# Expert layer on one core: tiles with one half of each factor, and 32 places instead of 64 for the longest list's second block

## The chip, the core and the metric

One core of a Trainium2 chip runs the whole program in one launch. The metric is the device time in microseconds (us), the median of several executions; lower is better. Engines are named as in the profile: PE is TensorE (PEld its loader of stationary operands), DVE VectorE, ACT ScalarE, SP the SyncE queue that issues nearly all transfers.

## The reference

Two layers of a backbone over 256 latent and 256 context tokens of width 1024. Layer 0 ends in a dense feed-forward part, layer 1 in eight experts of which each latent token takes two. The change touches the experts alone:

```python
def moe_swiglu(h, router, w1, w3, w2):
    logits = jnp.einsum('bld,de->ble', h, router).astype(F32)
    top_val, top_idx = lax.top_k(logits, TOP_K)
    top_w = jax.nn.softmax(top_val, axis=-1)
    gate = jnp.sum(jax.nn.one_hot(top_idx, N_EXPERTS, dtype=F32) * top_w[..., None], axis=-2)
    out = jnp.zeros(h.shape, F32)
    for e in range(N_EXPERTS):
        out = out + gate[..., e:e + 1] * swiglu(h, w1[e], w3[e], w2[e])
    return out.astype(h.dtype)
```

`swiglu` is (silu(h w1) * (h w3)) w2 with w1 and w3 of 1024 x 3584 and w2 of 3584 x 1024, all in fp32. The router of the reference, evaluated on its inputs, gives experts 0 to 7 lists of 53, 55, 63, 44, 38, 68, 48 and 143 tokens.

## The kernel before

**Stages.** Layer 0, the mixers of layer 1, then the experts (`experts`, L1302), which run alone at the end. Eight slots each take one expert: slot 0 is expert 0, slots 1 to 7 are the others by falling length of their lists. A slot gathers its tokens into columns (`gather`, L999) and runs seven steps; a step is one chunk of 512 hidden columns.

**Weights.** Every step needs six tiles of 128 x 2048 fp32 (1 MB): two for w1, two for w3 (tile 2 wi + kh holds the half kh of the contraction for factor wi), two for w2 (tile 4 + n holds output half n). They come from memory through a ring of nine buffers in the order of use (`raw`, L142), issued by SP. Nine are fetched before the stage starts (L1321). Every expert's weights are fetched whole: 8 x 7 x 6 = 336 tiles.

**Two ways to multiply.** `CAPS` and `SHORT` (L37, L38) say how many places a slot has, and `ORDER` and `ORDER_SHORT` in which sequence the steps of the slots run. Which of the two is taken is decided on the chip from the lists' lengths (L897 to L901, L1348).

- *Paired* slots (64 places; in `SHORT` slots 0 and 3 to 7) multiply in plain fp32 straight from the fetched tiles: the 64 columns of w1 and of w3 run side by side on two halves of the array (`up_pair`, L1107, matmul at L1113), a transpose and silu follow (`hidden_pair`, L1116), and the two output halves again run side by side (`down_pair`, L1128, L1134). Each fp32 matmul is two instructions in the trace.
- *Split* slots (slot 1 with blocks of 128 and 64 places, slot 2 with 128) multiply in three fp32r products. Each tile is first split into a high and a low part, in two halves of 1024 columns (`split`, L158: ACT at L170 makes the high part, DVE at L171 the low one); buffers for four such halves rotate. `up` (L1137, L1147) runs 12 matmuls per tile for a block of 128 places, and 8 for a block of 64, whose high and low activations lie side by side as one stationary operand of 128 columns. `hidden` (L1150) transposes and splits the result, `down` (L1177, L1184) multiplies by w2.

In the loop of `slots` (L1189) the second product of a step is issued inside the next step: after the first half of that step's first product comes `hidden` of the step before, then `ahead(…, 4, 5)`, which fetches and splits the two w2 tiles (where a split step is followed by a paired one), then the rest. The order on each engine's queue is set when the program is built, partly by a scheduler that moves instructions past each other. Each engine works its queue in order. Slot 1's second product is folded from two halves of rows by a matmul with a 0/1 matrix (`fold`, L1166).

Of the kernel before, what the change touches and what calls it, by code (L numbers as in the profile page):

```python
# [18 lines left out]
P = 128  # L19
# [10 lines left out]
NE = 8  # L30
# [40 lines left out]
NTA = P * len(_TA)  # L71
_TR = {n: i * P for i, n in enumerate(("iota", "iota64", "fold"))}
NTR = P * len(_TR)
# [9 lines left out]
class Net:  # L83
# [57 lines left out]

    def raw(self, src, n=2048):  # L142
# [718 lines left out]
    def route(self, l):  # L861
# [34 lines left out]
        nc.vector.tensor_add(ln, tot[:, 0], tot[:, 1])  # L896
        long = mk("long", [P, NE + 1])  # L897
        nc.vector.scalar_tensor_tensor(long[:, :NE], ln, 64.0, tab[:, P + 24:P + 32], ALU.is_gt, ALU.mult)
        nc.vector.reduce_sum(long[:, NE:], long[:, :NE], AX.X)
        self.long = mk("longi", [P, 1], I32)  # L900
        nc.vector.tensor_copy(self.long, long[:, NE:])  # L901

# [79 lines left out]
    def places(self, s, base, width):  # L982

        nc, mo = self.nc, self.mo
        G = mo.tile([P, 2, P], F32, tag="G", name=self.nm("G"), bufs=2)
        sp = mo.tile([P, 4], F32, tag="spb" if s == 1 else "sp", name=self.nm("spb"),
                     bufs=2 if s == 1 else 3)
        for tt in range(2):
            at = self.spos[tt][s]
            if base:  # L990
                nc.vector.tensor_scalar(sp[:, tt:tt + 1], at, float(-base), None, ALU.add)
                at = sp[:, tt:tt + 1]
            nc.vector.tensor_scalar(G[:, tt], self.t("iota" if width == P else "iota64"), at, None, ALU.is_equal)
        return G, sp

    def gather(self, s, base, width, first=False, whole=False):
# [7 lines left out]
        if whole:  # L1004
            xs = [mo.tile([P, KT, 64], F32, tag="xn", name=self.nm("xn"), bufs=2)]
        else:
            xs = [mo.tile([P, KT, P], F32R, tag=f"x{i}{big}{width if big else ''}", name=self.nm("xg"),
                          bufs=1 if big else 2) for i in range(2 if width == P else 1)]
        nk = 512 // width

        def activations(part):
            pool, tag = (self.hpp, "h") if part and first else (aux, "x")
            px = pool.tile([P, 512], F32, tag=tag, name=self.nm("px"))
            for k in range(nk):
                kk = part * nk + k
                for tt in range(2):
                    nc.tensor.matmul(px[:, k * width:(k + 1) * width], self.X[:, kk, NL + tt * P:NL + (tt + 1) * P],  # L1017
                                     G[:, tt, :width], start=tt == 0, stop=tt == 1)
            v = px.rearrange("p (k c) -> p k c", k=nk)
            sl = slice(part * nk, (part + 1) * nk)  # L1020
            if whole:
# [75 lines left out]
    def part(self, expert, j, i):  # L1097

        if isinstance(expert, int) and (j, i) in self.pre:
            return self.pre.pop((j, i))  # L1100
        return self.raw(self.I["moe"][expert, j, i])

    def parts(self, s, expert, j, i):
# [24 lines left out]
    def down_pair(self, expert, j, h, y):  # L1128

        mm = self.nc.tensor.matmul  # L1130
        ws = [self.part(expert, j, 4 + n) for n in range(2)]
        for f in range(4):
            for n in range(2):
                mm(y[64 * n:64 * n + 64], h[:, f], ws[n][:, f * 512:(f + 1) * 512],  # L1134
                   start=j == 0 and f == 0, stop=j == NCH - 1 and f == 3)
# [14 lines left out]
    def hidden(self, acts):  # L1150
# [24 lines left out]
    def down(self, s, expert, j, n, parts, y, first, last):  # L1175

        mm = self.nc.tensor.matmul  # L1177
        ws = self.parts(s, expert, j, 4 + n)
# [11 lines left out]
    def slots(self, l, steps, order, caps, base=0, first=False):  # L1190
# [60 lines left out]
        for i, (s, j) in enumerate(steps):  # L1251
# [20 lines left out]
            if split:  # L1272
                self.up(s, order[s], j, 0, 1, blocks, pss)
                for ps, b in zip(pss, blocks):
                    a = mo.tile([P, 512], F32, tag="act", name=self.nm("act"), bufs=4)
                    nc.scalar.activation(a, ps, AF.Silu if len(b[0]) > 1 else AF.Copy)
                    acts.append([a])
# [5 lines left out]
                for a, ps, b in zip(acts, pss, blocks):  # L1283
                    if len(b[0]) > 1:
                        nc.vector.tensor_mul(a[0], a[0], ps)
                    else:
                        a.append(mo.tile([P, 512], F32, tag="act", name=self.nm("act"), bufs=4))
                        nc.vector.tensor_copy(a[1], ps)
            else:
                self.up_pair(order[s], j, 1, blocks[0][0][0], pss[0])  # L1290
# [17 lines left out]
    def experts(self, cx, l, ps):  # L1308
# [38 lines left out]

        long = nc.values_load(self.long[0:1, 0:1], min_val=0, max_val=NE + 2)  # L1348
        with tc.If(long < 3, preferred_fallthrough_block=True) as c:
# [71 lines left out]
def _constants():  # L1421
# [10 lines left out]
    for name, d in (("r64", 64), ("r32", 32)):  # L1432
# [6 lines left out]
        tab[:, _TA[name]:][:, :P] = r  # L1439
    tr[:, _TR["iota64"]:][:, :P] = i[None, :] % 64  # L1440
    tr[:, _TR["fold"]:][:, :64] = i[:, None] % 64 == np.arange(64)[None, :]
    ts[:, P:P + 8] = np.arange(8)
    ts[:, P + 8:P + 16] = [1e7, 700, 600, 500, 400, 300, 200, 100]
# [114 lines left out]
```

## Time and profile before

| | |
|---|---|
| median of 3 runs | 1982.26 us (1972.82 to 1993.71) |
| the profiled execution, its own time | 1975.04 us |
| its span, first to last instruction | 1973.2 us |
| mean granted clock of TensorE | 0.982 |
| expert stage in the span, first gather to the last product | 984.5 to 1950 us |
| transfers in the program | 478.45 MB, 242 GB/s over the span |

The span is what the rows below divide; 1.84 us of the execution lie around it. Times in a row of the timeline are from the span's start. A row of the timeline gives start, length, engine, line, operation, tiles and the number of instructions merged; the length runs to the end of the last one, so the step from one row's start to the next row's is what the work occupies on PE.

### The profile page before, as it was taken

The numbers are of one execution on the slowest core, as the hardware profiler recorded it, in microseconds if no ns is written. First come the engines' busy times: TensorE is split into PE (matmuls) and PEld (weight loads), VectorE is DVE, ScalarE is ACT, GpSimd is POOL, SyncE is SP. The second block draws the span as 40 slices with busy tenths as digits, with TensorE's granted clock in tenths as the row PEclk, the third lists the DMA queues.
The fourth block names the chain that finished last, engine by engine and source line by source line (L and its number), as shares of the span: only waits on it lengthen the run. The fifth ranks groups of instructions, "written<-read, shape, count | busy, mean of one in ns | idle before, by whom it ended". The sixth has DMA issues, their size and how long they took to land.

```text
span 1973.2 us, 22813 instructions
## 1 busy us (share of the span) xinstructions
PE 1883.8 (95%) x8918; PEld 1177.6 (60%) x8918; DVE 835.8 (42%) x1633; ACT 665.4 (34%) x1059; POOL 0.2 (0%) x4
## 2 busy tenths in 40 slices
PE   6999999999999999999699999999999999998995
PEld 4866546778888878665656545454455455444552
DVE  6586455533333347865423323322342223223262
ACT  4475234422222225854322312221332223212231
POOL 0000000000000000000000000000000000000000
PEclk9999999999999999999899999999999999999998
DMA  7320345442332224225578987998998998998972
GB/s 301 137 76 22 118 186 217 159 150 74 122 108 79 72 91 171 98 108 202 217 286 336 364 347 296 420 418 331 421 404 345 420 375 318 409 368 328 418 306 81
DMA packets 68811, 478.45 MB, mean 242 GB/s; under 512 B 7760, under 2 KB 8912, under 8 KB 13392
## 3 DMA queue, kind: packets, MB, share of 16 engines
q1 hardware_dynamic: 68112, 473.04, 61.0%
q10 hardware_dynamic: 576, 3.80, 0.5%
q8 instruction: 74, 1.21, 0.2%
q14 instruction: 49, 0.40, 0.1%
HBM read 475.76 MB, written 1.05 MB: 242 GB/s over the span
## 4 chain that ended last, share of the span: by engine, by line
PE 93%; DMA 3%; DVE 2%; ACT 1%; issue 0%; SPq 0%; ACTq 0%; DVEq 0%
PE ph L1113 17%; PE ph L1147 11%; PE y L1134 8%; PE pf L184 6%; PE pf L186 6%; PE pf L185 6%; PE y L1184 6%; PE pp L186 3%; PE pp L185 3%; PE pp L184 3%; PE ada L211 2%; PE px L1017 2%; PE ds L664 2%; PE po L184 1%; DMA raw<-in_ada 1%; PE po L185 1%
## 5 line engine op out<-in xcount | busy, mean ns | idle before, releaser
L171 DVE TENSOR_TENSOR w<-raw,w 128x1024 fp32r<-128x1024 f32 (+2 forms) x310 | 353.4, 1166 | 295.5 <-ACT w L170 295.1
L170 ACT ACTIVATE w<-raw 128x1024 fp32r<-128x1024 f32 (+2 forms) x310 | 302.5, 1009 | 287.3 <-PE pf L186 152.6
L1113 PE MATMUL ph<-raw,xn 128*64 128x512 f32 x1344 | 354.4, 608 | 0.0
L1147 PE MATMUL ph<-w,xg 128*128 128x512 f32 x896 | 224.8, 403 | 4.1 <-DVE w L171 4.1
L1113 PEld LDWEIGHTS ph<-raw,xn 128*64 128x64 f32 x1344 | 99.5, 138 | 182.5 <-issue 179.8
L1147 PEld LDWEIGHTS ph<-w,xg 128*128 128x128 f32 x896 | 165.6, 190 | 63.2 <-issue 15.3
L1134 PE MATMUL y<-raw,hn 128*64 128x512 f32 x672 | 173.8, 601 | 0.0
L184 PE MATMUL pf<-fhhi,w 128*128 128x512 f32 x352 | 137.2, 391 | 1.5 <-ACT fhhi L315 1.5
L185 PE MATMUL pf<-fhlo,w 128*128 128x512 f32 x352 | 137.1, 389 | 0.0
L186 PE MATMUL pf<-fhhi,w 128*128 128x512 f32 x352 | 137.0, 389 | 0.0
L112 ACT ACTIVATE act<-ph 128x512 f32<-128x512 f32 x42 | 25.1, 597 | 279.7 <-PE ph L1113 279.7
L1184 PE MATMUL y<-w,hh 128*128 128x512 f32 x336 | 105.5, 411 | 7.4 <-DVE yacc L1242 3.8
L1134 PEld LDWEIGHTS y<-raw,hn 128*64 128x64 f32 x672 | 52.2, 138 | 93.9 <-issue 92.8
L184 PE MATMUL pp<-hhi,w 128*128 128x512 f32 (+1 forms) x272 | 104.0, 382 | 0.0
L186 PE MATMUL pp<-hhi,w 128*128 128x512 f32 (+1 forms) x272 | 102.8, 378 | 0.0
L185 PE MATMUL pp<-hlo,w 128*128 128x512 f32 (+1 forms) x272 | 101.7, 374 | 0.0
L1125 DVE TENSOR_TENSOR hn<-hn,ht 128x256 f32<-128x256 f32 x42 | 17.6, 418 | 190.6 <-ACT hn L1124 190.6
L1184 PEld LDWEIGHTS y<-w,hh 128*128 128x128 f32 x336 | 61.4, 190 | 43.6 <-issue 16.0
L184 PEld LDWEIGHTS pf<-fhhi,w 128*128 128x128 f32 x352 | 66.0, 188 | 18.4 <-issue 2.5
L185 PEld LDWEIGHTS pf<-fhlo,w 128*128 128x128 f32 x352 | 66.1, 188 | 13.8 <-DVE fhlo L316 0.3
L186 PEld LDWEIGHTS pf<-fhhi,w 128*128 128x128 f32 x352 | 66.1, 188 | 13.8
L185 PE MATMUL pf<-ulo,w 128*128 128x512 f32 x176 | 68.5, 389 | 0.0
(326 smaller groups left out, 2440.9 us busy)
## 6 DMA issues: line engine op xcount, KB each, us to landing
raw<-in_moe SPq DMA_DIRECT2D x336, 1024.0 KB, 8.9
raw<-in_ada SPq DMA_DIRECT2D x45, 1024.0 KB, 4.9
raw<-in_ffn SPq DMA_DIRECT2D x22, 1024.0 KB, 4.8
raw<-in_win SPq DMA_DIRECT2D x16, 1024.0 KB, 4.8
raw<-in_ffn SPq DMA_DIRECT2D x16, 704.0 KB, 4.0
raw<-in_wout SPq DMA_DIRECT2D x8, 1024.0 KB, 4.9
raw<-in_winv SPq DMA_DIRECT2D x7, 640.0 KB, 4.8
raw<-in_ada ACTq DMA_DIRECT2D x3, 1024.0 KB, 7.7
```

The costliest lines, as they stand in the source:

```text
L170: self.nc.scalar.activation(hi[:, :m], t[:, c:c + m], AF.Copy)
L171: self.nc.vector.tensor_sub(lo[:, :m], t[:, c:c + m], hi[:, :m].bitcast(F32))
L184: mm(out, llo, rhi, start=first, stop=False)
L185: mm(out, lhi, rlo, start=False, stop=False)
L186: mm(out, lhi, rhi, start=False, stop=last)
L211: nc.tensor.matmul(st["ps"][32 * j:32 * j + 32, :], self.sc[:, k, :], w[:, j * 512:(j + 1) * 512], start=k == 0, stop=k == KT - 1)
L664: nc.tensor.matmul(ps[:, :w], q[j][r:r + 32, q0:q0 + P], k[j][r:r + 32, k0:k0 + w], start=True, stop=True, tile_position=(r, 0))
L1017: nc.tensor.matmul(px[:, k * width:(k + 1) * width], self.X[:, kk, NL + tt * P:NL + (tt + 1) * P], G[:, tt, :width], start=tt == 0, stop=t ...
L1113: mm(ps[64 * wi:64 * wi + 64], x[:, 4 * kh + kk], ws[wi][:, kk * 512:(kk + 1) * 512], start=kh + kk == 0, stop=kh == 1 and kk == 3)
L1134: mm(y[64 * n:64 * n + 64], h[:, f], ws[n][:, f * 512:(f + 1) * 512], start=j == 0 and f == 0, stop=j == NCH - 1 and f == 3)
L1147: mm(ps, xs[x][:, 4 * kh + kk], ws[kk // 2][i][:, kk % 2 * 512:(kk % 2 + 1) * 512], start=kh == 0 and (x, i, kk) == todo[0], stop=kh == 1 ...
L1184: mm(yn, hs[x][:, f], ws[f // 2][i][:, f % 2 * 512:(f % 2 + 1) * 512], start=first and (x, i, f) == todo[0], stop=last and (x, i, f) == to ...
```

## The change

1. `SHORT` gives the second block of slot 1 32 places instead of 64. That block's products are no longer split: four plain fp32 matmuls of 32 stationary columns run side by side on four strips of the array, one for each of four slices of the contraction, from the fetched tile itself. Their four partial results stand below one another and are summed by the fold (now four strips onto 32 columns). Block one of slot 1 (128 places) still uses the split parts of the same tile, so a tile of slot 1 is now in use until the four plain matmuls have read it.
2. A tile of a paired slot now holds half of the slices of both factors (or of both output halves): two pieces of 128 x 1024 from two tiles of the old layout, 4 KB per partition each. Layout in memory is unchanged; so are the bytes and the count of transfers.
3. The choice of the order also asks whether a list is longer than 160 (then it takes `CAPS`). A table of 128 columns is added.

```diff
-SHORT = ((64,), (128, 64), (128,), (64,), (64,), (64,), (64,), (64,))
+SHORT = ((64,), (128, 32), (128,), (64,), (64,), (64,), (64,), (64,))
...
-        self.dq().dma_start(t[:, :n], src)
+        dst = t[:, :n]
+        if shape:
+            dst = dst.rearrange("p (a c) -> p a c", a=shape[0])
+        self.dq().dma_start(dst, src)
...
+        nc.vector.tensor_scalar(long[:, NE:2 * NE], ln, float(sum(SHORT[1])), 3.0, ALU.is_gt, ALU.mult)
...
+        if width == 32:
+
+            xs = [xs[0][:, :, :32].bitcast(F32), None, None]
+        nk = min(512 // width, KT)
...
     def parts(self, s, expert, j, i):
 
-        return self.ready.pop((s, j, i), None) or self.split(self.part(expert, j, i))
+        if (s, j, i) in self.ready:
+            return self.ready.pop((s, j, i))
+        t = self.part(expert, j, i)
+        return t, self.split(t)
+
+    def both(self, expert, j, i):
+
+
+        if isinstance(expert, int) and (j, i) in self.pre:
+            return self.pre.pop((j, i))
+        w = self.I["moe"][expert, j]
+        h = slice(i % 2 * 1024, (i % 2 + 1) * 1024)
+        src = w[i // 2:i // 2 + 3:2, :, h] if i < 4 else w[4:6, :, h]
+        return self.raw(src.rearrange("w p c -> p w c"), shape=(2, 1024))
 
     def up_pair(self, expert, j, kh, x, ps):
 
         mm = self.nc.tensor.matmul
-        ws = [self.part(expert, j, 2 * wi + kh) for wi in range(2)]
-        for kk in range(4):
-            for wi in range(2):
-                mm(ps[64 * wi:64 * wi + 64], x[:, 4 * kh + kk], ws[wi][:, kk * 512:(kk + 1) * 512],
-                   start=kh + kk == 0, stop=kh == 1 and kk == 3)
+        for t in range(2):
+            w = self.both(expert, j, 2 * kh + t)
+            for kk in range(2):
+                for wi in range(2):
+                    c = wi * 1024 + kk * 512
+                    mm(ps[64 * wi:64 * wi + 64], x[:, 4 * kh + 2 * t + kk], w[:, c:c + 512],
+                       start=kh + t + kk == 0, stop=kh + t + kk == 3)
...
-        ws = self.parts(s, expert, j, 2 * wi + kh)
+        t, ws = self.parts(s, expert, j, 2 * wi + kh)
         for ps, (xs, *_) in zip(pss, blocks):
+            if len(xs) == 3:
+                for kk in range(4):
+                    mm(ps[32 * kk:32 * kk + 32], xs[0][:, 4 * kh + kk], t[:, kk * 512:(kk + 1) * 512],
+                       start=kh == 0, stop=kh == 1)
+                continue
...
+                if len(a) == 3:
+                    for q in range(2):
+                        for i in range(4):
+                            nc.tensor.matmul(pt[:, q * P + i * 32:q * P + (i + 1) * 32], a[q][:, i * P:(i + 1) * P],
+                                             self.t("fold")[:, 64:96], start=True, stop=True)
+                    h = hh[:, :, :32].bitcast(F32)
+                    v = pt[:, :256].rearrange("p (q f c) -> p q f c", q=2, f=4)
+                    nc.scalar.activation(h, v[:, 0], AF.Silu)
+                    nc.vector.tensor_mul(h, h, v[:, 1])
+                    parts.append((h, None, None))
+                    continue
...
+            if len(hs) == 3:
+                for f in range(4):
+                    mm(yn[32 * f:32 * f + 32], hs[0][:, f], t[:, f * 512:(f + 1) * 512], start=first, stop=last)
+                continue
...
-        pre = {(i // 6, j): self.raw(self.I["moe"][0, i // 6, j]) for i, j in enumerate((0, 2, 1, 3, 4, 5, 0, 2, 1))}
+        pre = {(i // 6, i % 6): self.both(0, i // 6, i % 6) for i in range(9)}
```

`down_pair` is changed as `up_pair` is. Lines of the changed kernel lie some 3 to 43 lines further down: L1113 becomes L1133, L1134 L1156, L1147 L1175, L1159 L1187, L1184 L1227; the plain matmuls of 32 columns are L1169 and L1222.

**Order on PE, first place.** One tile of slot 1 (w3, first half), before: `xg_7397` and `xg_7398` are the high and low activations of the block of 128, `xg_7406` those of the second block, `w_...` a split half of the tile.

```order
L1147 MATMUL ph_8956<-w_8959,xg_7397 128x512 x2
L1147 MATMUL ph_8956<-w_8959,xg_7398 128x512
...
L1147 MATMUL ph_8956<-w_8962,xg_7397 128x512 x2
L1147 MATMUL ph_8956<-w_8962,xg_7398 128x512
...
L1147 MATMUL ph_8957<-w_8959,xg_7406 128x512 x4
L1147 MATMUL ph_8957<-w_8962,xg_7406 128x512 x4
```

The same tile now; `raw_7240` is the fetched tile itself.

```order
L1175 MATMUL ph_8894<-w_8897,xg_7398 128x512 x2
L1175 MATMUL ph_8894<-w_8897,xg_7399 128x512
...
L1175 MATMUL ph_8894<-w_8900,xg_7398 128x512 x2
L1175 MATMUL ph_8894<-w_8900,xg_7399 128x512
...
L1169 MATMUL ph_8895<-raw_7240,xg_7407 32x512 x4
```

Eight matmuls of 128 columns from split parts became four of 32 columns from the raw tile.

**Order on PE, second place.** The end of a step of slot 2 inside the paired step that follows, before: `ht_8697` is the transposed hidden block of slot 2, `hh_8698` its high part made by ACT from it, `w_8707` the first split half of the w2 tile, and `ph_8686` the first product of the paired step.

```order
L1147 MATMUL ph_8620<-w_8654,xg_7804 128x512
L1113 MATMUL ph_8686<-raw_7237,xn_7945 64x512
L1159 MATMUL ht_8697<-tab,act_8618 128x128 x4
L1113 MATMUL ph_8686<-raw_7238,xn_7945 64x512
...
L1184 MATMUL y_8102<-w_8707,hh_8698 128x512 x2
L1184 MATMUL y_8102<-w_8707,hl_8703 128x512
```

The same place now:

```order
L1175 MATMUL ph_8566<-w_8600,xg_7777 128x512
L1133 MATMUL ph_8632<-raw_7238,xn_7918 64x512 x4
L1133 MATMUL ph_8632<-raw_7239,xn_7918 64x512 x4
L1187 MATMUL ht_8643<-tab,act_8564 128x128 x4
L1227 MATMUL y_8075<-w_8653,hh_8644 128x512 x2
L1227 MATMUL y_8075<-w_8653,hl_8649 128x512
```

Before, one of the eight plain matmuls of the paired step stands alone ahead of the transposes, and seven between them and the second product; now all eight stand ahead of the transposes. The program's paired matmuls (1008 in the stage) stand in runs between other work; 86 runs held one without its partner of the other half of the array before, 20 do now. Of the seven steps of slot 2, six had the seven matmuls in between before and the last had none; now none of the seven has any. On ACT the queue is the same in both kernels at this place:

```order
L1319 ACTIVATE act_8564<-ph_8531 128x512
L173 ACTIVATE w_8597<-raw_7237 128x1024
L173 ACTIVATE w_8600<-raw_7237 128x1024
L182 ACTIVATE hh_8644<-ht_8643 128x512
L173 ACTIVATE w_8653<-raw_7240 128x1024
L173 ACTIVATE w_8656<-raw_7240 128x1024
```

These rows are of the changed kernel: the high part of the hidden block is made first, the halves of the w2 tile behind it.

## Rows read from the trace of the kernel before

**Rows 1.** The page, part 1: busy time, share of the span, instructions.

```profile
PE 1883.8 (95%) x8918; PEld 1177.6 (60%) x8918; DVE 835.8 (42%) x1633; ACT 665.4 (34%) x1059; POOL 0.2 (0%) x4
```

**Rows 2.** The page, part 4: the chain that ended last, shares by engine.

```profile
PE 93%; DMA 3%; DVE 2%; ACT 1%; issue 0%; SPq 0%; ACTq 0%; DVEq 0%
```

**Rows 3.** Windows, expert stage: length, busy per engine, clock, DMA share, GB/s.

```profile
984.50:1950.00 965.50, 938.43 (x4178) 492.41 (x4178) 309.31 (x431) 249.55 (x337) 0.00 (x0) 0.98 0.88 356
```

**Rows 4.** Waits of the SP queue: total us, times, longest.

```profile
SPq L149 <- DVE w L171: 669.3, 97, 39.1
SPq L149 <- PE ph L1113: 422.7, 141, 10.5
```

**Rows 5.** Lines by form: busy us, mean ns of one, idle before them.

```profile
L1113 PE MATMUL ph<-raw,xn 128*64 128x512 f32 x1344 | 354.4, 608 | 0.0
L1147 PE MATMUL ph<-w,xg 128*128 128x512 f32 x896 | 224.8, 403 | 4.1 <-DVE w L171 4.1
```

**Rows 6.** Timeline of PE in a step of slot 1: start, us, what.

```profile
1186.76 9.56 PE L1147 MATMUL ph<-w,xg 128*128 128x512 f32 x40
1196.25 3.65 PE L1134 MATMUL y<-raw,hn 128*64 128x512 f32 x16
1199.84 0.50 PE L1147 MATMUL ph<-w,xg 128*128 128x512 f32 x1
```

**Rows 7.** Timeline of PE: four fp32 products of 32 columns side by side, elsewhere.

```profile
919.51 1.06 PE L211 MATMUL ada<-raw,sc 128*32 128x512 f32 x8
920.51 0.66 PE L632 MATMUL ptp<-tab,ap 128*128 128x128 f32 x4
...
926.86 1.92 PE L211 MATMUL ada<-raw,sc 128*32 128x512 f32 x16
```

**Rows 8.** Timeline, second product of slot 2 with plain matmuls ahead of it.

```profile
1266.50 1.07 PE L1113 MATMUL ph<-raw,xn 128*64 128x512 f32 x2
1267.51 0.66 PE L1159 MATMUL ht<-tab,act 128*128 128x128 f32 x4
1268.09 3.65 PE L1113 MATMUL ph<-raw,xn 128*64 128x512 f32 x14
1271.67 0.73 PE L1184 MATMUL y<-w,hh 128*128 128x512 f32 x2
...
1268.69 3.89 ACT L170 ACTIVATE w<-raw 128x1024 fp32r<-128x1024 f32 x4
...
1269.78 4.63 DVE L171 TENSOR_TENSOR w<-raw,w 128x1024 fp32r<-128x1024 f32 x4 [0.26 <-ACT w L170]
```

**Rows 9.** Timeline, the same place in the last step of slot 2.

```profile
1808.09 0.33 PE L1159 MATMUL ht<-tab,act 128*128 128x128 f32 x1
1811.31 0.72 PE L1184 MATMUL y<-w,hh 128*128 128x512 f32 x2 [2.89 <-DVE w L171]
...
1808.95 3.88 ACT L170 ACTIVATE w<-raw 128x1024 fp32r<-128x1024 f32 x4
...
1810.03 4.63 DVE L171 TENSOR_TENSOR w<-raw,w 128x1024 fp32r<-128x1024 f32 x4 [0.25 <-ACT w L170]
```

**Rows 10.** Windows behind that wait, PE alone: length, busy, clock, DMA share, GB/s.

```profile
1812.20:1815.60 3.40, 3.40 (x10) 0.50 1.01 410
```

**Rows 11.** DMA, 1400 to 1450 us: the queue's packets, MB, share of 16 engines.

```profile
q1 hardware_dynamic: 2881, 20.98, 101.1%
```

**Rows 12.** DMA, 867.5 to 868.5 us: a tile with 4 KB per partition.

```profile
DMA packets 104, 0.41 MB, mean 414 GB/s; under 512 B 3, under 2 KB 3, under 8 KB 104
...
q1 hardware_dynamic: 104, 0.41, 101.9%
```

**Rows 13.** The page, part 6: issues, KB each, median us to landing.

```profile
raw<-in_moe SPq DMA_DIRECT2D x336, 1024.0 KB, 8.9
...
raw<-in_win SPq DMA_DIRECT2D x16, 1024.0 KB, 4.8
...
bd<-in_lrubd SPq DMA_DIRECT2D x2, 512.0 KB, 3.7
```

More of the change, by code (lines that the diff above doesn't have):

```diff
@@ L71 @@
 NTA = P * len(_TA)
-_TR = {n: i * P for i, n in enumerate(("iota", "iota64", "fold"))}
+_TR = {n: i * P for i, n in enumerate(("iota", "iota64", "iota32", "fold"))}
 NTR = P * len(_TR)
@@ L140, in dq, with raw @@
         return self.nc.scalar if self.ndq <= 8 and self.ndq % 2 else self.nc.sync
-    def raw(self, src, n=2048):
+    def raw(self, src, n=2048, shape=None):
         if self.ring:
@@ L896, in route @@
         nc.vector.tensor_add(ln, tot[:, 0], tot[:, 1])
-        long = mk("long", [P, NE + 1])
+        long = mk("long", [P, 2 * NE + 1])
         nc.vector.scalar_tensor_tensor(long[:, :NE], ln, 64.0, tab[:, P + 24:P + 32], ALU.is_gt, ALU.mult)
-        nc.vector.reduce_sum(long[:, NE:], long[:, :NE], AX.X)
+        nc.vector.tensor_scalar(long[:, NE:2 * NE], ln, float(sum(SHORT[1])), 3.0, ALU.is_gt, ALU.mult)
+        nc.vector.reduce_sum(long[:, 2 * NE:], long[:, :2 * NE], AX.X)
         self.long = mk("longi", [P, 1], I32)
-        nc.vector.tensor_copy(self.long, long[:, NE:])
+        nc.vector.tensor_copy(self.long, long[:, 2 * NE:])
         pm = mk("pm", [P, 2, NE])
@@ L992, in places @@
                 at = sp[:, tt:tt + 1]
-            nc.vector.tensor_scalar(G[:, tt], self.t("iota" if width == P else "iota64"), at, None, ALU.is_equal)
+            nc.vector.tensor_scalar(G[:, tt], self.t({P: "iota", 64: "iota64", 32: "iota32"}[width]), at, None, ALU.is_equal)
         return G, sp
@@ L1006, in gather @@
         else:
-            xs = [mo.tile([P, KT, P], F32R, tag=f"x{i}{big}{width if big else ''}", name=self.nm("xg"),
+            xs = [mo.tile([P, KT, P], F32R, tag=f"x{i}{big}{max(width, 64) if big else ''}", name=self.nm("xg"),
                           bufs=1 if big else 2) for i in range(2 if width == P else 1)]
-        nk = 512 // width
+        if width == 32:
+            xs = [xs[0][:, :, :32].bitcast(F32), None, None]
+        nk = min(512 // width, KT)
         def activations(part):
@@ L1018, in activations @@
                                      G[:, tt, :width], start=tt == 0, stop=tt == 1)
-            v = px.rearrange("p (k c) -> p k c", k=nk)
+            v = px[:, :nk * width].rearrange("p (k c) -> p k c", k=nk)
             sl = slice(part * nk, (part + 1) * nk)
-            if whole:
+            if whole or width == 32:
                 self.acopy(xs[0][:, sl], v)
@@ L1097, in part, with parts @@
     def part(self, expert, j, i):
+        return self.raw(self.I["moe"][expert, j, i])
+    def parts(self, s, expert, j, i):
+        if (s, j, i) in self.ready:
[3 more added lines that the diff above has]
+    def both(self, expert, j, i):
         if isinstance(expert, int) and (j, i) in self.pre:
             return self.pre.pop((j, i))
-        return self.raw(self.I["moe"][expert, j, i])
-    def parts(self, s, expert, j, i):
-        return self.ready.pop((s, j, i), None) or self.split(self.part(expert, j, i))
+        w = self.I["moe"][expert, j]
+        h = slice(i % 2 * 1024, (i % 2 + 1) * 1024)
+        src = w[i // 2:i // 2 + 3:2, :, h] if i < 4 else w[4:6, :, h]
+        return self.raw(src.rearrange("w p c -> p w c"), shape=(2, 1024))
     def up_pair(self, expert, j, kh, x, ps):
         mm = self.nc.tensor.matmul
-        ws = [self.part(expert, j, 2 * wi + kh) for wi in range(2)]
-        for kk in range(4):
-            for wi in range(2):
-                mm(ps[64 * wi:64 * wi + 64], x[:, 4 * kh + kk], ws[wi][:, kk * 512:(kk + 1) * 512],
-                   start=kh + kk == 0, stop=kh == 1 and kk == 3)
+        for t in range(2):
[5 more added lines that the diff above has]
+                       start=kh + t + kk == 0, stop=kh + t + kk == 3)
     def hidden_pair(self, a):
@@ L1130, in down_pair @@
         mm = self.nc.tensor.matmul
[L1131 to L1135, printed above, removed]
+        for t in range(2):
+            w = self.both(expert, j, 4 + t)
+            for f in range(2):
+                for n in range(2):
+                    c = n * 1024 + f * 512
+                    mm(y[64 * n:64 * n + 64], h[:, 2 * t + f], w[:, c:c + 512],
+                       start=j == 0 and t + f == 0, stop=j == NCH - 1 and t + f == 2)
     def up(self, s, expert, j, wi, kh, blocks, pss):
@@ L1177, in down @@
         mm = self.nc.tensor.matmul
-        ws = self.parts(s, expert, j, 4 + n)
+        t, ws = self.parts(s, expert, j, 4 + n)
         for b, hs in enumerate(parts):
             yn = y(b)
+            if len(hs) == 3:
+                for f in range(4):
+                    mm(yn[32 * f:32 * f + 32], hs[0][:, f], t[:, f * 512:(f + 1) * 512], start=first, stop=last)
+                continue
             todo = [(x, i, f) for x in range(len(hs)) for i in range(2) for f in range(4) if x + i < 2]
@@ L1275, in slots @@
                     a = mo.tile([P, 512], F32, tag="act", name=self.nm("act"), bufs=4)
-                    nc.scalar.activation(a, ps, AF.Silu if len(b[0]) > 1 else AF.Copy)
+                    nc.scalar.activation(a, ps, AF.Silu if len(b[0]) == 2 else AF.Copy)
                     acts.append([a])
@@ L1283, in slots @@
                 for a, ps, b in zip(acts, pss, blocks):
-                    if len(b[0]) > 1:
+                    if len(b[0]) == 2:
                         nc.vector.tensor_mul(a[0], a[0], ps)
@@ L1288, in slots @@
                         nc.vector.tensor_copy(a[1], ps)
+                        if len(b[0]) == 3:
+                            a.append(None)
             else:
@@ L1346, in all_slots @@
             self.finish()
-        long = nc.values_load(self.long[0:1, 0:1], min_val=0, max_val=NE + 2)
+        long = nc.values_load(self.long[0:1, 0:1], min_val=0, max_val=NE + 2 + 9)
         with tc.If(long < 3, preferred_fallthrough_block=True) as c:
@@ L1440, in _constants @@
     tr[:, _TR["iota64"]:][:, :P] = i[None, :] % 64
+    tr[:, _TR["iota32"]:][:, :P] = i[None, :] % 32
     tr[:, _TR["fold"]:][:, :64] = i[:, None] % 64 == np.arange(64)[None, :]
+    tr[:, _TR["fold"] + 64:][:, :32] = i[:, None] % 32 == np.arange(32)[None, :]
     ts[:, P:P + 8] = np.arange(8)
```

## The prediction

> **What bounds the kernel now.** I read the page's engine table first, then the chain, then the expert stage by windows, then the waits of the transfer queue. PE is busy for 95% of the span [rows 1], and the chain of work that ended last is 93% PE and 3% transfers [rows 2]: PE sets the end. The change touches the expert stage alone, and there in 965.5 us PE is busy for 938.4, while the transfers fill 0.88 of the 16 DMA engines' time [rows 3]. So PE bounds the stage, with the transfers close behind. In a full stretch the queue moves 20.98 MB in 50 us, 420 GB/s, at 101.1% of the engines [rows 11]: 2.50 us for a tile of 1.0486 MB, 840 us for 336 tiles. SP mostly waits for a buffer to come free, 669 us in all behind a split on DVE and 423 us behind paired products [rows 4]; a fetched tile is there in time, and the two big groups of PE show idle of 0.0 and 4.1 us [rows 5]. Work taken from PE here can shorten the stage, as long as no new wait appears on PE and the tiles still come.
>
> **The 32 places.** In slot 1 each of 42 tiles (7 steps of 6) had 8 matmuls of 128 columns for the second block. In such a step 40 of them occupy PE from 1186.76 to 1196.25 us [rows 6], 9.49 / 40 = 0.237 us each, 1.90 us per tile. In their place comes a group of four plain fp32 matmuls of 32 columns side by side. The program has that form in another part: a lone group (eight instructions, as an fp32 matmul is two) starts at 919.51 and the next work at 920.51, 1.00 us; two groups in a row take 1.92 us against 1.06 for one, so the second adds 0.86 [rows 7]. In the new order each group stands alone between matmuls of other widths, so I take 1.00. The gain is 0.90 us per tile, 37.7 us for 42 (43.6 with 0.86). The fold keeps its 8 matmuls per step; ACT and DVE lose a few short operations, beside PE's work and worth nothing. The splits stay, as the block of 128 needs them.
>
> The Trainium skill's page "TensorE: Matmul & The Clock Gate" (Part 3, measured speedup) has three products of 32 columns side by side at 2.38 times the speed of one after the other. Four at the same share, 0.79, would by an estimate from that page take 1.08 us where the ideal is 0.86, and the gain would be 34.4 us instead of 37.7. The rows with four side by side decide here.
>
> **Whole pairs.** Paired matmuls share the array: eight of them (16 instructions) run from 1196.25 to 1199.84, 3.59 us or 0.90 per pair [rows 6]. One without its partner takes as long as a pair: the lone one from 1266.50 to 1267.51 took 1.01, and the seven that follow 3.58, from 1268.09 to 1271.67, as much as eight [rows 8]. Where the order tears a pair apart, half a pair's time, 0.45, is lost at each of the two runs. A tile with both factors is enough for whole pairs, so the order has no reason to start one half early: by the count of runs 86 held an odd matmul and 20 do now. 66 x 0.45 = 29.5 us. The bounds are nothing, if the halves that are torn apart fill gaps that PE would have had anyway, and 66 x 0.55 = 36 with a lone one at 1.01.
>
> **What the new order adds.** The second product of a slot 2 step needs the transposed hidden block, of which ACT makes the high part, and the split halves of the w2 tile, which stand behind that operation on ACT's queue in both kernels. Before, PE has cover: after the transposes at 1267.51 the seven plain matmuls run from 1268.09, meanwhile ACT starts on the halves at 1268.69 and DVE at 1269.78, and the product starts at 1271.67 without a wait [rows 8]. The diff does not say so, but in the new order those matmuls stand ahead of the transposes, in all seven steps of slot 2 (second place of the order). The trace before shows the price already, because its last step of slot 2 had no cover: the last transpose at 1808.09, ACT's halves from 1808.95, DVE's from 1810.03, and PE idle for 2.89 us until 1811.31 [rows 9]. One step of seven paid that, now seven do: 6 x 2.89 = 17.3 us. Queued on PE behind the waiting matmul are the rest of the product and the next paired products; ACT waits for those, with nothing else to do.
>
> **The clock.** From 1812.2 to 1815.6 us, behind that wait, the granted clock is 0.50, the lower of its two levels (1.2 of 2.4 GHz), with PE full [rows 10]: 3.4 us for 1.7 us of work. The new waits are alike, so I count 6 x 1.7 = 10.2 us. The bounds are nothing and two such stretches each, 20.4.
>
> **The transfers.** Two things load the queue. First, a tile of slot 1 used to be free once DVE had split it; now four matmuls must have read it too, for a w2 tile those behind the transposes and the fold of the next step. SP issues in order, so all later tiles wait. The trace has no such hold: from below it costs nothing, from above one landing, 8.9 us [rows 13], in each of seven steps, 62 us. Second, 252 tiles come in pieces of 4 KB per partition. A tile of that kind moved 414 GB/s at 101.9% of the engines [rows 12], 2.2% less per busy time than 420 at 101.1%: 2.55 us. From the other side, 512 KB at 4 KB per partition land in 3.7 us and 1024 KB at 8 KB in 4.8 [rows 13]; with 2.50 us of flow in the latter 2.3 are fixed, which leaves 1.4 for half a tile, 2.80 for a whole one. I take 2.55, the direct measure: the queue needs 252 x 2.55 + 84 x 2.50 = 853 us, which the shorter stage of some 935 still covers, with less to spare. Together I take one landing, 9 us, nearer to the lower end, as PE hardly waits for tiles now.
>
> **The sum.** -37.7 - 29.5 + 17.3 + 10.2 + 9 = -30.7 us. Against the profiled execution's own 1975.0 us (its span 1973.2 and 1.8 around) that is 1944. The median of the three runs is 1982.3, 7.2 above that execution, so the predicted median is 1952. A measurement of this kernel tells about 1%, 20 us, from no change: the forecast is outside that, by little.
>
> **Rivals.** *The new waits cost nothing.* While PE stands, the queue fills buffers, and later waits go instead. For it: stretches at the full 420 GB/s [rows 11]. Against it: PE has hardly any such waits now [rows 2], so little can be given back. -37.7 - 29.5 + 9 = -58: 1924. Chance 0.12.
>
> *The torn pairs cost nothing now*, because each odd half fills a gap that stays. For it: the order starts it early only where PE's next work was thought to be waiting. Against it: both parts of the torn pair are followed at once by other work [rows 8]. -30.7 + 29.5 = -1: 1981. Chance 0.14.
>
> *The transfers become the bound.* The two pieces of a tile come from places 1 or 2 MB apart, which no row shows. At 2.80 us a tile the queue is busy for 916 us; with the seven holds of 8.9 us and some 25 us at the stage's ends (nine tiles are there at its start) it needs 1003 us, 38 more than now: 2020. With those stops it is slower than before from (965.5 - 87 - 210) / 252 = 2.65 us a tile on. For it: 0.88 used already. Against it: the 414 GB/s [rows 12]. Chance 0.14. The skill's page "DMA: Bandwidth & Descriptors" (Latency and other measured facts) reports copies whose rows lie 2 MiB apart at 164 GB/s where 214 is full rate; there the distance is between partitions, here between the two pieces of each. By an estimate from that page a tile would take 3.25 us and the kernel some 150 us more; no row here bears it out.
>
> *It does not do what it says.* If the other order ran, slots 0 and 3 would leave the paired way: 72 matmuls of 0.237 against 12 pairs of 0.90, some 6 us in each of 14 steps, 85 us slower. The longest list has 143 tokens, under 160: chance 0.02.
>
> **How the numbers follow.** The forecast, 1952, has 0.58; its own range, with the bounds of the clock, the groups and half of the holds, is 1936 to 1974. The range for 8 in 10 takes in the first two rivals in part: 1922 to 1996; left out are the bound transfers, the other order and the lower half of the first rival. Faster by over 1% (under 1962): the first rival and four fifths of the forecast, 0.60. Slower by over 1% (above 2002): 0.13. Within: 0.27.
>
> **What would show it.** Right: 336 instructions of 32 columns in groups of about 1.00 us; hardly a lone paired matmul left on PE's timeline; seven waits of about 2.9 us before slot 2's second product, ended by the split on DVE, where one was; a lower mean granted clock than 0.982 in the stage; transfers at 0.91 of the engines. Wrong: no such waits, or the clock staying up after them (nearer 1924); PE waiting for paired tiles with the engines full (the pieces cost more); a group above 1.3 us; the same busy time of the paired groups, 354 us in the first product [rows 5], with the pairs whole.

## The result, and the profile after

The changed kernel takes 1944.69 us (median of 4 runs, 1940.58 to 1950.19), the kernel before 1981.51 in the same comparison: ratio 0.9834, 95% interval 0.9802 to 0.9867, by which it is some 33 us faster (the two medians lie 36.8 us apart). The forecast was 1952.

PE's busy time and the chain, from the page of the changed kernel, answer to [rows 1] and [rows 2]:

```profile
PE 1830.0 (94%) x8918; PEld 1122.1 (58%) x8918; DVE 832.3 (43%) x1626; ACT 664.3 (34%) x1052; POOL 0.2 (0%) x4
...
PE 13%; DVE 1%; ACT 0%; issue 0%; DMA 0%; ACTq 0%; DVEq 0%
```

The chain is lost early here (14% of the span in all), so the stage is read by windows instead. The expert stage as [rows 3] has it:

```profile
985.50:1915.10 929.60, 881.31 (x4173) 434.42 (x4175) 305.40 (x423) 248.38 (x330) 0.00 (x0) 0.97 0.93 370
```

It is 35.9 us shorter. PE is busy for 57.1 us less, but idle for 48.3 instead of 27.1, and the transfers fill 0.93 of the engines' time instead of 0.88. Lines by form, PE alone, the first two answer to [rows 5]:

```profile
L1133 PE MATMUL ph<-raw,xn 128*64 128x512 f32 x1344 | 320.5, 601 | 0.0
L1175 PE MATMUL ph<-w,xg 128*128 128x512 f32 x672 | 178.6, 416 | 17.8 <-DVE w L174 17.8
L1227 PE MATMUL y<-w,hh 128*128 128x512 f32 x224 | 81.0, 439 | 18.3 <-DVE w L174 17.6 <-ACT hh L182 0.7
L1169 PE MATMUL ph<-raw,xg 128*32 128x512 f32 x224 | 29.8, 605 | 0.0
```

Paired products cost less; a split matmul costs more (416 ns against 403); idle time stands before the split matmuls of the first product (L1175) and of the second (L1227). A group of four on PE's timeline occupies 0.99 us, 1179.48 to 1180.47:

```profile
1179.48 1.07 PE L1169 MATMUL ph<-raw,xg 128*32 128x512 f32 x8
...
1180.47 0.66 PE L1141 MATMUL ht<-tab,act 128*128 128x128 f32 x4
```

The second product of slot 2, where [rows 8] had cover:

```profile
1124.69 0.66 PE L1187 MATMUL ht<-tab,act 128*128 128x128 f32 x4
...
1125.39 0.60 ACT L182 ACTIVATE hh<-ht 128x512 fp32r<-128x512 f32 x1 [11.05 <-PE ht L1187]
1125.88 3.88 ACT L173 ACTIVATE w<-raw 128x1024 fp32r<-128x1024 f32 x4
...
1128.24 1.22 PE L1227 MATMUL y<-w,hh 128*128 128x512 f32 x2 [2.89 <-DVE w L174]
```

ACT had been waiting for 11 us and makes the halves after the hidden block; PE waits for 2.89 us, as in [rows 9]. Windows of PE behind such a wait, at two of the six places; the granted clock is the third number from the end, half of full speed at the first place and full at the second:

```profile
1263.80:1267.20 3.40, 3.40 (x9) 0.50 1.02 408
1787.20:1790.60 3.40, 3.40 (x15) 1.00 1.02 407
```

What SP waits for, against [rows 4]:

```profile
SPq L152 <- DVE w L174: 646.9, 94, 39.1
SPq L152 <- PE ph L1133: 235.1, 130, 6.1
...
SPq L152 <- PE ph L1169: 88.7, 25, 4.7
SPq L152 <- PE y L1222: 86.8, 12, 11.4
```

The last two are new: 176 us in which the queue stood behind tiles that the plain matmuls of 32 columns still had to read. And a tile is sometimes late:

```profile
1430.38 2.00 ACT L173 ACTIVATE w<-raw 128x1024 fp32r<-128x1024 f32 x2 [3.46 <-DMA raw<-in_moe]
...
1432.84 1.40 PE L1175 MATMUL ph<-w,xg 128*128 128x512 f32 x5 [3.07 <-DVE w L174]
```

### The profile page after: what moved, and what is told of

Its sections match the earlier page's. It is cut to its first block, busy times and chain, and to the rows that moved or that the text cites. A ratio compares the mean times of both kernels' runs of the same rounds, so it can differ in the third digit from the quotient of the medians.

```text
span 1939.3 us, 22842 instructions
## 1 busy us (share of the span) xinstructions
PE 1830.0 (94%) x8918; PEld 1122.1 (58%) x8918; DVE 832.3 (43%) x1626; ACT 664.3 (34%) x1052; POOL 0.2 (0%) x4
## 5 line engine op out<-in xcount | busy, mean ns | idle before, releaser
L1133 PE MATMUL ph<-raw,xn 128*64 128x512 f32 x1344 | 320.5, 601 | 0.0
L1175 PE MATMUL ph<-w,xg 128*128 128x512 f32 x672 | 178.6, 416 | 17.8 <-DVE w L174 17.8
L1133 PEld LDWEIGHTS ph<-raw,xn 128*64 128x64 f32 x1344 | 89.8, 137 | 172.0 <-issue 169.5
L1175 PEld LDWEIGHTS ph<-w,xg 128*128 128x128 f32 x672 | 127.1, 196 | 71.9 <-issue 30.4
L1156 PE MATMUL y<-raw,hn 128*64 128x512 f32 x672 | 155.2, 596 | 0.0
L1145 DVE TENSOR_TENSOR hn<-hn,ht 128x256 f32<-128x256 f32 x42 | 17.6, 418 | 194.2 <-ACT hn L1144 194.2
L1156 PEld LDWEIGHTS y<-raw,hn 128*64 128x64 f32 x672 | 46.4, 137 | 93.0 <-issue 91.1
L1227 PE MATMUL y<-w,hh 128*128 128x512 f32 x224 | 81.0, 439 | 18.3 <-DVE w L174 17.6
L189 PEld LDWEIGHTS pf<-fhhi,w 128*128 128x128 f32 x352 | 66.1, 188 | 13.8
L187 PE MATMUL pf<-uhi,w 128*128 128x512 f32 x176 | 68.5, 389 | 0.0
```

The lines of the kernel that those rows point to most:

```text
L187: mm(out, llo, rhi, start=first, stop=False)
L189: mm(out, lhi, rhi, start=False, stop=last)
L1133: mm(ps[64 * wi:64 * wi + 64], x[:, 4 * kh + 2 * t + kk], w[:, c:c + 512], start=kh + t + kk == 0, stop=kh + t + kk == 3)
L1145: nc.vector.tensor_mul(h, h, v[:, :, 1])
L1156: mm(y[64 * n:64 * n + 64], h[:, 2 * t + f], w[:, c:c + 512], start=j == 0 and t + f == 0, stop=j == NCH - 1 and t + f == 2)
L1175: mm(ps, xs[x][:, 4 * kh + kk], ws[kk // 2][i][:, kk % 2 * 512:(kk % 2 + 1) * 512], start=kh == 0 and (x, i, kk) == todo[0], stop=kh == 1 ...
```

## The experiments

Ratios are to the kernel before, which ran beside each. Runs one to four stood beside one another, so did five to eight and nine to eleven; inside such a group medians are compared, from group to group ratios.

**The changed kernel again.** No edit.

> The changed kernel once more, beside the three that follow, on the same chip. Both theories: 0.983 of the kernel before (0.980 to 0.987), a mean clock near 0.975, six idle times of 2.89 us of PE before the second product of slot 2.

Measured 1947.61 us, before 1974.60: 0.9842 (0.9806 to 0.9878), as expected. The waits before slot 2's second product are the same in its profile, 17.6 us in all.

**Slot 2's high part behind the first w2 tile's split.**

```diff
...
+            if late and len(state[todo[0]]["blocks"]) == 1:
+                n = len(self.acts)
                 ahead(todo[0], todo[1], 4, 5)
+                with self.tc.issue_after(self.acts[n + 1].ins):
+                    todo = hidden(todo)
...
```

`acts` lists the ACT operations of the splits, so that `hidden` comes behind the second half of the first w2 tile; the condition holds for slot 2 alone, which has one block.

> Only the place of one ACT operation in slot 2 is changed: the high part of the transposed hidden block stands behind the two halves of the first w2 tile instead of ahead of them (seven steps). Theory A, the exposed wait costs its length and the half clock behind it: the six waits of 2.89 us fall to 0.7 or less and five of the six half-clock stretches of 3.4 us behind them go, 13 + 8.5 = 21 us less than the changed kernel, ratio to the kernel before near 0.973. Theory B, PE is held by the transfers now and idle time only moves: the waits go here and come back as waits for late tiles, 0 to 5 us less, ratio 0.981 to 0.984.

Measured 1939.05 us, 8.6 less than the changed kernel beside it; 0.9805 (0.9768 to 0.9842). Waits of PE:

```profile
PE y L1228 <- ACT hh L183: 5.5, 7, 1.4
...
PE y L1157 <- DMA raw<-in_moe: 3.7, 6, 0.7
PE ph L1134 <- DMA raw<-in_moe: 2.2, 4, 0.6
```

The 18.3 us became 5.5, as theory A has it, and the half-clock stretches in the stage went from 47.8 to 30.7 us. But 5.9 us came back as waits of paired matmuls for late tiles; the changed kernel has none in its profile above and 1.7 us in the one taken beside this run. The result lies between the two theories: the wait was real, and part of it moves to the transfers.

**Both factors in one piece of memory.** The arrangement of the weights is changed so that `both` fetches one contiguous tile, and `part` two pieces:

```diff
...
-        return self.raw(self.I["moe"][expert, j, i])
...
+        src = w[2 * (i % 2):2 * (i % 2) + 2, :, h] if i < 4 else w[4:6, :, h]
+        return self.raw(src.rearrange("w p c -> p w c"), shape=(2, 1024))
...
```

> The expert weights are laid out in memory so that a tile with both factors lies in one piece of 8 KB per partition; the 84 tiles of the split slots come in two pieces of 4 KB instead. PE's work and order are as in the changed kernel. Theory A, pieces of 4 KB cost 2% of the transfer's time: queue time falls by 252 x 0.05 - 84 x 0.05 = 8 us, the waits of PE that end with a late tile (four, 8.9 us in the changed kernel) shrink by half or more, 4 to 9 us less than the changed kernel. Theory B, the late tiles come from the order and from buffers held, not from the size of a piece: same waits, within 3 us.

Measured 1945.11 us, 2.5 less than the changed kernel, inside the scatter; idle time before the first split products 17.0 against 18.8 us. Of that, what ends with a late tile fell from 10.4 to 8.2 us, not by half. Theory B: the size of the pieces isn't the main reason why tiles are late.

**No tile held.**

```diff
...
-                    mm(ps[32 * kk:32 * kk + 32], xs[0][:, 4 * kh + kk], t[:, kk * 512:(kk + 1) * 512],
+                    mm(ps[32 * kk:32 * kk + 32], xs[0][:, 4 * kh + kk],
+                       ws[kk // 2][0][:, kk % 2 * 512:(kk % 2 + 1) * 512].bitcast(F32),
...
```

The same is done for w2.

> The four plain matmuls of 32 columns read the high parts of the tile instead of the tile itself (so slot 1's second block is computed with weights of reduced precision); the fetched tile is free again when its split is done, as in the kernel before. Same count and length of matmuls. Theory A, the held buffers make tiles late: the waits of SP behind these matmuls (175 us in the changed kernel) go, the four late tiles too, 9 us less than the changed kernel. Theory B, the tiles are late because the queue is full: same late tiles, within 3 us.

Measured 1940.03 us, 7.6 less than the changed kernel; 0.9814 (0.9774 to 0.9855). Idle time before the split first products fell from 18.8 to 12.7 us, its share that ends with a late tile from 10.4 to 3.6, and SP no longer waits behind the plain matmuls of 32 columns. Theory A in its mechanism. Its size is loose: three of the six runs took 1934 to 1935 us, the other three 1945 to 1947, and those of the changed kernel 1943 to 1950.

**Each part alone.** The 32 places without the pair tiles, and the pair tiles without the 32 places. The main lines, against the changed kernel; what belongs to the part that is left out goes with them:

```diff
...
-        for t in range(2):
-            w = self.both(expert, j, 2 * kh + t)
...
+        ws = [self.part(expert, j, 2 * wi + kh) for wi in range(2)]
...
```

```diff
-SHORT = ((64,), (128, 32), (128,), (64,), (64,), (64,), (64,), (64,))
+SHORT = ((64,), (128, 64), (128,), (64,), (64,), (64,), (64,), (64,))
```

> Only the 32 places of slot 1's second block; the paired slots keep tiles of one factor. Theory A, the parts add as in the prediction's sum: the plain groups of four bring 37 us, the order still has seven paired matmuls behind the transposes of slot 2, so no new waits there and no further half-clock stretches, eight more runs with an odd paired matmul cost 4, held tiles up to 9: 24 to 33 us less than before, ratio 0.983 to 0.988. Theory B, the two parts need each other (the time that one gives back is lost again in torn pairs and late tiles unless the other is there): 10 us or less, ratio 0.995 or more.

Measured 1978.96 us, before 1974.22: 1.0024 (0.9999 to 1.0049). No gain at all: theory B's outcome.

> Only the tiles that hold both factors; slot 1's second block keeps 64 places and split products. The order has no matmul behind the transposes of slot 2 in six of seven steps. Theory A, as in the prediction's sum: whole pairs bring 27 us (60 runs with an odd matmul less, 0.45 each), five more waits of 2.89 and the half clock behind them take back 14 + 8: 0 to 8 us less, ratio 0.996 to 1.000, six idle times of 2.89 us in the trace. Theory B, torn pairs cost more than half a pair's time each and the waits are given back: 20 us less or more, ratio 0.990 or below.

Measured 1979.88 us: 1.0029 (1.0008 to 1.0049). No gain either, rather 0.3% of loss; the six waits of theory A are there, its 0 to 8 us less are not. So the parts bring nothing one by one and 33 us together. The stage of the four kernels, from its first matmul to ACT's last `yh`, by what occupies PE (the step from each matmul's start to the next one's, less idle time, added up over the timeline):

| us | before | 32 places alone | pairs alone | changed |
|---|---|---|---|---|
| paired products | 496.5 | 497.5 | 467.1 | 462.1 |
| split products | 333.8 | 259.6 | 348.7 | 268.3 |
| groups of four | 0 | 51.4 | 0 | 42.9 |
| idle | 27.0 | 45.5 | 41.6 | 47.8 |
| all the rest | 105.5 | 108.6 | 106.0 | 105.7 |
| stage | 962.8 | 962.6 | 963.4 | 926.8 |

Pairs alone: 29.4 us less in paired products, as reckoned, and 14.9 more in split ones (half clock) and 14.6 more idle. Waits of PE there:

```profile
PE y L1199 <- DVE w L174: 17.3, 6, 2.9
...
PE ph L1162 <- DVE w L174: 11.6, 7, 2.7
```

The 32 places alone: the split products and groups fall by 22.8 in all, and 18.5 us of idle time stand against it, half of that before paired products, which before waited for nothing:

```profile
PE ph L1123 <- DMA raw<-in_moe: 4.8, 5, 1.3
PE y L1144 <- DMA raw<-in_moe: 4.5, 5, 1.3
```

The groups cost 51.4 us there, not 42, mainly because the order tears eight of the 42 apart, here three and one:

```profile
1192.93 1.06 PE L1157 MATMUL ph<-raw,xg 128*32 128x512 f32 x6
1193.92 3.08 PE L1163 MATMUL ph<-w,xg 128*128 128x512 f32 x12
1196.92 1.05 PE L1157 MATMUL ph<-raw,xg 128*32 128x512 f32 x2
1197.90 1.07 PE L1123 MATMUL ph<-raw,xn 128*64 128x512 f32 x2
```

Three products side by side occupy 0.99 us, the single one 0.98.

**Plain matmuls first.**

```diff
-        for ps, (xs, *_) in zip(pss, blocks):
+        for ps, (xs, *_) in sorted(zip(pss, blocks), key=lambda b: -len(b[1][0])):
```

> The changed kernel with slot 1's plain matmuls of 32 columns ahead of the split ones of the same tile in the first product (28 tiles). They need the fetched tile alone, so PE has 1.0 us of work while ACT and DVE split, and the tile is free as early as its split is done. Theory A, held tiles and exposed first splits: the idle time before the split matmuls of the first product falls from 18.8 to 12.7 us or less (what it was without the hold), SP's waits behind the plain matmuls of the first product (89 us) go, 5 to 9 us less than the changed kernel, ratio near 0.980. Theory B, idle time only moves to paired tiles: within 3 us of the changed kernel.

Measured 1953.17 us; 0.9888 (0.9862 to 0.9914), no gain. The ratio of the changed kernel, 0.9842 (0.9806 to 0.9878), is lower, but the intervals overlap. SP's waits behind these matmuls fell from 90 to 31 us. The idle time before the first products did fall to 13.5 us, but before the second ones it rose from 17.6 to 22.4, and 6.1 us came before matmuls that read fetched tiles. Theory B in its mechanism; whether the edit loses time is not shown.

**Three edits together.** The diffs of the second, third and seventh run on the changed kernel.

> Three edits together on the changed kernel: slot 2's high part behind the first w2 tile's split, plain matmuls of 32 columns first, and the layout with both factors in one piece. Theory A, each gain stands by itself: 8.5 + 6 + 2.5 us less than the changed kernel, 1930 us, ratio 0.976. Theory B, the transfers bound the stage once PE waits less: no more than the first edit alone, 1938 us, ratio 0.980, with idle time of PE before paired matmuls that end with a late tile.

Measured 1939.85 us; 0.9812 (0.9785 to 0.9839): no more than the first edit alone (0.9805). That is theory B's outcome, but its cause, the transfers, is not shown: one of the three edits brought no gain by itself. And in the profiled execution, the median one, 27.3 us at half clock lie ahead of the stage, in a part that the edits don't touch, where the second run has 13.6; the stage itself is 4.8 us shorter than in the second run.

**The cover for the pairs alone.** The diff of the second run on the sixth.

> The tiles with both factors alone, as before with 64 places in slot 1, and the high part of slot 2's transposed block behind the first w2 tile's split. Theory A, the pairs alone brought nothing because the exposed waits and the half clock behind them took as much as whole pairs gave (29 us of paired products against 15 of idle time and 15 of slower split products): with the cover back both shrink by two thirds, 15 to 22 us less than the tiles alone, ratio 0.992 to 0.995 or below. Theory B, something else holds the pairs alone (the smaller pieces, the transfers): within 5 us of them, ratio 1.000 to 1.003.

Measured 1962.46 us, before 1975.47: 0.9943 (0.9920 to 0.9966), by the ratios 17 us less than the pairs alone. Theory A. The wait before the second product is down to 4.8 us, the half-clock stretches in the stage from 44 to 17 us:

```profile
PE ph L1163 <- DVE w L175: 16.1, 9, 3.1
...
PE y L1200 <- ACT hh L183: 4.8, 7, 0.7
```

**No tile held, for the 32 places alone.** The diff of the fourth run on the fifth.

> The 32 places alone, with the plain matmuls reading the high part of the split tile (so that block is computed with weights of reduced precision) and the fetched tile free when its split is done. Theory A, the 32 places alone brought nothing because held tiles make later ones late (18 us more idle time): the waits for late paired tiles (9 us) and for late splits go, 10 to 18 us less than the 32 places alone, ratio 0.993 to 0.997. Theory B, paired tiles of one factor are late because PE needs two of them, 2 MB, before it can go on, and groups of four are torn by the same order: the idle time before paired products stays, within 5 us, ratio 1.000 to 1.004.

Measured 1965.38 us: 0.9954 (0.9929 to 0.9979), 13.8 us (0.7%) less than the 32 places alone, by the ratios. Theory A. Idle time in the stage fell from 45.5 to 35.4 us; no paired matmul of PE waits for a tile any more, and the largest waits left are on splits:

```profile
PE y L1217 <- DVE w L174: 7.3, 5, 2.9
PE ph L1164 <- DVE w L174: 6.8, 6, 2.1
```

**Cover and layout.** The diffs of the second and third run on the changed kernel.

> The changed kernel with the slot 2 edit of the second run and the layout of the third, without the plain matmuls first. Theory A, the small gains add: 8.5 + 2.5 us less than the changed kernel, ratio 0.979, near 1934 where the kernel before stands at 1974. Theory B, the layout brings nothing: as the second run, 0.9805.

Measured 1935.23 us, before 1975.47: 0.9792 (0.9761 to 0.9824). By its median it is the fastest version here that keeps full precision; its interval overlaps that of the cover alone, so the layout's share is not shown.

**The same without the hold.** With the diff of the fourth run besides.

> The eleventh run's kernel (slot 2's high part behind the first w2 tile's split, both factors in one piece of memory) with slot 1's plain matmuls reading the high part of the split tile, so that block is computed with weights of reduced precision and no fetched tile is held. It tells what the hold still costs in the fastest version. Theory A, it costs there what it cost in the changed kernel, 8 us: ratio near 0.975. Theory B, with the waits of slot 2 gone and the tiles in one piece the hold is hidden: within 3 us, ratio 0.978 to 0.980.

Measured 1920.62 us, before 1982.12: 0.9721 (0.9689 to 0.9752), 0.7 points or 14 us below the eleventh run, more than theory A had. The wait on first splits is 13.3 us instead of 18.5 and the paired products wait for 1.6 us instead of 4.5:

```profile
PE ph L1177 <- DVE w L175: 13.3, 9, 3.1
...
PE y L1157 <- DMA raw<-in_moe: 1.6, 3, 0.7
```

## Why the prediction was right

The stage fell by 36.0 us in the table above, the sum had 30.7. The four mechanisms that were priced are all in the trace: the groups, the whole pairs, the exposed waits and the half clock behind them. Term by term, in the changed kernel:

- **The 32 places.** 37.7 forecast. 336 split matmuls at 0.237 are 79.6 us, and the 42 groups take 42.9: 36.7. The group of 1.00 us from the other part of the program [rows 7] held; the 1.08 estimated from the Trainium skill's page "TensorE: Matmul & The Clock Gate" (Part 3, measured speedup) was too dear.
- **Whole pairs.** 29.5 forecast, paired products fell by 34.4. Some 5 of these are the clock: by the timeline 36 instructions of paired matmuls lay in half-clock stretches before, 414 ns each instead of 243, and 6 do now. The other 29.4 is the term. The pairs alone show 29.4 in all; there 13 such instructions lie at half clock, so that some 26 are left for 60 torn runs less, against 27 by 0.45 each.
- **The exposed waits.** 17.3 forecast, 14.7 measured (17.6 less the 2.9 of before). Six steps of slot 2 wait for 2.89 us, not seven: in the last one two splits stand ahead of the hidden block, and PE waits for 0.69 and 0.28.
- **The clock.** 10.2 forecast. The granted clock of the stage, behind its first gather, is at half for 37.5 us in ten stretches, before for 20.5 in five: 17.0 more, of which half is lost, 8.5. Five of the six waits were followed by one; the sixth, at 1787, was not.
- **The transfers.** 9 forecast. Idle time before split first products rose from 4.1 to 17.8 us. About half of it, 8.9 us in four waits, ends with a tile that came late, as the one at 1432.84; the rest with a first split that stands in ACT's or DVE's queue behind other work, of a gather for instance, which the sum did not have. By the fourth run the hold is worth 7.6 us, by the third the pieces 2.5, not told from nothing; the two terms of the forecast were a landing, 9 us, for both, chosen between bounds of 0 and 62 us. That a term of this width came so near is luck.
- **Not foreseen.** The kernel before had waits on the accumulator (3.8 us) and on the copy ahead of the transposes of paired steps (4.1, now 0.7), lines by form:

```profile
L1184 PE MATMUL y<-w,hh 128*128 128x512 f32 x336 | 105.5, 411 | 7.4 <-DVE yacc L1242 3.8 <-DVE w L171 2.9 <-ACT hh L179 0.7
...
L1121 PE MATMUL ht<-tab,act 128*128 128x128 f32 x168 | 27.6, 283 | 4.1 <-ACT act L112 4.1
```

That is 7.2 us gone, which more than makes good the 4.7 us of idle time beyond the 9 of the forecast. Two further slips of the prediction are without weight: the first rival and four fifths of the forecast give a chance of 0.58, not 0.60, and the transfers took 0.93 of the engines, not 0.91.

Of the rivals, *the new waits cost nothing* fell: the waits are there, and with the cover the time drops, though by 8.6 us and not by 21. *The torn pairs cost nothing* fell in its mechanism, since the paired products did get 29 us shorter; that the gain needn't reach the end is what the pairs alone show. *The transfers become the bound* fell as the outcome, but they are close: in the stage PE and the transfers are now both at 0.93 or more, and where the cover took a wait from PE, some of it returned as late tiles.

What the sum did not say is that its terms are no separate worths. The same terms, taken for the 32 places alone, gave the expectation of 24 to 33 us less, and none came; so that the sum holds for both parts together is in part luck. Added up, the parts alone give +0.4 us in the stage, together they give -36.0. The 36.4 between lie, by the table, in idle time (18.5 + 14.6 alone, 20.8 together: 12.3), whole groups of four (8.5), split products (against the 0.248 us per matmul of before, 9.2 + 14.9 more alone and 17.9 together: 6.2, mostly the clock), the paired products (6.0) and the rest (3.4). Idle time is the largest, and 9.3 us of it are the waits of paired products for tiles, which the 32 places alone have and the changed kernel hasn't (1.7 us in its second profile). The ninth and tenth run show a part of what held each: the waits behind slot 2's transposes the pairs, the held tiles the 32 places. With these out of the way the stage is some 15 us shorter than before in either (by the ratios 11 and 9 us in all), where the terms have 27 and 37; what takes the rest was not tested. That a tile with both factors lets PE go on after 1 MB instead of 2, and so hides late tiles in the changed kernel, fits the fact that it has no such wait; it was not tried by itself, so the cause of the joint gain is in that part argued.

## What to carry to other kernels

Here each of two edits measured as nothing, and together they gained 33 us: where PE and the transfers are both near nine tenths of the stage or above, price edits together as well as alone. Before work is moved ahead of a dependent product, look at what it was covering, and if the consumer's other inputs are ready early, put their making ahead of the late one in its queue. An extra reader of a buffer in a ring is a cost in the ring, here 8 to 14 us for 42 tiles (the lower figure loosely), that no engine's busy time shows.

## What the runs showed of the hardware

A plain fp32 product of 32 columns without its three neighbours occupies PE for 0.98 us, nearly as long as four side by side, 1.00 (eight torn groups in the 32 places alone).

Transfers in pieces of 4 KB per partition take more busy time of the engines, by how much differs from kernel to kernel. The queue's packets, MB and share of the engines from 1000 to 1880 us, before, in the changed kernel, in the pairs alone, and in the eleventh run, in this order:

```profile
q1 hardware_dynamic: 44923, 327.18, 91.5%
```

```profile
q1 hardware_dynamic: 76305, 335.64, 96.3%
```

```profile
q1 hardware_dynamic: 74123, 325.78, 95.9%
```

```profile
q1 hardware_dynamic: 57063, 337.33, 94.9%
```

Per busy time that is 406, 396, 386 and 404 GB/s. Three quarters of the tiles come in two pieces in the second and third, a quarter in the last. So the transfers are 2.5% dearer in the changed kernel and 5% in the pairs alone; why the same pieces cost twice as much there is not shown. Where all of it is put on the tiles in pieces, they cost 3% more in the changed kernel and 7% in the pairs alone; the 2.2% read from one tile [rows 12] lies below both. In the changed kernel a tile takes 1.0486 MB / 396 GB/s = 2.65 us of busy time on average, some 2.67 one in pieces, which is where the rival of the bound transfers had the kernel slower. It isn't, because that rival counted 62 us of holds where the fourth run shows 7.6, and the end hardly feels the pieces (third run). The 3.25 us a tile estimated from the Trainium skill's page "DMA: Bandwidth & Descriptors" (Latency and other measured facts) didn't come about: that would be 30% more than 2.50.
